# A two-layer encoder trunk on one core: shorter inverse-root chains, and seven-product pairs placed anew in the feed-forward products

## The chip, the cores and the metric

The kernel runs on one core of a Trainium2 chip. The metric is device time in microseconds (us) of one execution; lower is better. A core has five engines with queues of their own: TensorE (PE, with its weight loads PEld), VectorE (DVE), ScalarE (ACT), GpSimd (POOL) and SyncE (SP), which here issues most of the transfers from memory.

## The reference, cut to what matters

256 tokens of width 2048 go through two layers. All is float32. Each layer has an input projection, two kinds of attention, an output projection, and a gated feed-forward part with inner width 5632. Norms stand before and after each part.

```python
def rms_norm(x, g):
    y = xf * lax.rsqrt(jnp.mean(xf * xf, axis=-1, keepdims=True) + EPS)
    return y * g

def swiglu(h, w_gate, w_up, w_down):
    return (jax.nn.silu(h @ w_gate) * (h @ w_up)) @ w_down

for l in range(DEPTH):                      # DEPTH = 2
    h = rms_norm(x, pre_mix_norm[l])
    m = hybrid_mixer(h, l, ...)             # h @ w_in, attention, @ w_o
    x = x + rms_norm(m, post_mix_norm[l])
    h = rms_norm(x, pre_ffn_norm[l])
    f = swiglu(h, w_gate[l], w_up[l], w_down[l])
    x = x + rms_norm(f, post_ffn_norm[l])
return x
```

## The kernel before, in words

**Splitting.** Every float32 factor is written as the sum of two rounded parts, hi and lo. ACT makes hi by a copy (L250), DVE makes lo as the rest (L252). One product of a 128x128 block with a 128x512 block is then three matmuls: hi by hi, hi by lo, lo by hi (function product, L925 to L927; in down also L1135 to L1138, and L1187 to L1189 in its tail).

**Pairs.** Weights arrive in units of 256 rows by 512 columns, one 512 KB load each. A K pair (kp) is 256 rows; there are 8 of them in the input, gate and up products (2048 rows) and 22 in down (5632 rows). The 256 tokens are two tiles of 128 (t = 0, 1). A pair of two weight units (gate and up of one column block, or two column blocks of down) and two token tiles is a 2x2 by 2x2 block product. Done plainly it takes eight products, 24 matmuls. Some pairs are done with seven products, 21 matmuls (seven_products, L942). Such a pair needs sums of weight blocks and of token blocks:

- The weight sums come from mixed_weights (L216). The second unit, T, is loaded by SP and then half of the first unit is added onto it by an accumulating load that POOL issues (L210, L211). DVE then forms a difference in T (L232) and two sums in G (L233), and ACT and DVE split all of it (L225, L226).
- The token sums come from token_sums (L929): four 128x128 operations on DVE and a split (sh on L937, sl on L939). In gate and up, pair_sums (L1028) adds hi and lo first (L1032); the result is kept for all column blocks of the layer.
- Some partial products are shared by several outputs. They go into four banks of their own (p1, p6, p7, q5); after the last seven-product pair of a block, shared_part (L959) moves them to SBUF in one ACT copy and four DVE steps (L963 to L966), which frees the banks.

**Loops.** In the feed-forward part, 11 column blocks c of gate and up run one after the other, each over 8 K pairs. The pairs done with seven products are 2, 4, 5, 6 (SEVEN), in block 0 only 4 and 6 (FIRST_SEVEN, with another order of pairs, FIRST_ORDER). FORM_AT says behind which pair of block 0 the token sums of which pair are built. Then down runs in two halves (two column blocks of 512 each) over 22 pairs; DOWN_SEVEN lists the pairs with seven products, the same in both halves. The last three pairs of half 1 are done by token tile and column block (TAIL), so that tile 0 can be finished while tile 1 is still multiplied.

**Banks.** PSUM has eight banks: four (acc) and four (b and o). Blocks alternate: one set holds a block's sums, the other its shared partial products, and the next block's sums take over the set of the shared products.

**After the products.** evac_chunk (mixer) and evac_sum (down) take a bank's sum, square it with an accumulated total on ACT, and multiply it by the norm's gain on DVE. rescale (L484) adds the four totals, takes the inverse root (rsqrt, L362: logarithm and exponential on ACT, then one Newton step of five DVE operations) and updates x in four blocks of 512 columns (L490). The result is stored (L498) at the end, or transposed for the next part.

**Order.** Loads of weights go in a fixed order through SP's queue, each as soon as its buffer is free: four buffers for ordinary units (raw), three for G, four for T in gate and three in down; six of each split part (hi, lo). A planner orders each engine's queue by priorities; every engine then runs its queue strictly in order.

Of the kernel before, what the change touches and what calls it, by code (L numbers as in the profile page):

```python
# [9 lines left out]
F32 = mybir.dt.float32  # L10
F32R = mybir.dt.float32r
BF16 = mybir.dt.bfloat16
AF = mybir.ActivationFunctionType
# [4 lines left out]
P = 128  # L18
# [32 lines left out]

def lambda_init(layer):
    return 0.8 - 0.6 * math.exp(-0.3 * layer)


def weight_order():

    order = []

    def queue_pair(name, l, kp, c):  # L60
        order.append((name, l, kp, c))
        return len(order) - 1

    plan = []
    sevens, plain = set(), set()
    for l in range(L):
        lay = {"in": {}, "o": {}, "gate": {}, "up": {}, "down": {}}
        for n, (ca, cb) in enumerate(PAIRS):
            for kp in IN_ORDER if n else range(KT // 2):
                lay["in"][ca, kp] = queue_pair("w_in", l, kp, ca)  # L70
                lay["in"][cb, kp] = queue_pair("w_in", l, kp, cb)
                if kp in IN_NOW[n]:
                    plain.add(lay["in"][cb, kp])
        order_o = [(c, kp) for kp in KP_O for c in (0, 1)]
        order_o += [(c, kp) for c in (2, 3) for kp in range(KT // 2)]
        lay["order_o"] = order_o
        for c, kp in order_o:
            lay["o"][c, kp] = queue_pair("w_o", l, kp, c)
        for c in range(FF // CW):
            for kp in FIRST_ORDER if c == 0 else range(KT // 2):  # L80
                lay["gate"][c, kp] = queue_pair("w_gate", l, kp, c)
                lay["up"][c, kp] = queue_pair("w_up", l, kp, c)
                if kp in (FIRST_SEVEN if c == 0 else SEVEN):
                    sevens.add(lay["up"][c, kp])
        for half in range(2):
            for kp in range(FF // P // 2):
                for c in (2 * half, 2 * half + 1):
                    lay["down"][c, kp] = queue_pair("w_down", l, kp, c)
                if kp in DOWN_SEVEN:
# [51 lines left out]
def kernel(  # L141
# [220 lines left out]
    def rsqrt(dst, src, inv, nm):  # L362
        n = dst.shape[-1]
        m = small.tile([P, 2, 4], F32, tag="rsq", bufs=4, name=f"rsq_{nm}")
        u, ms = m[:, 0, 0:n], m[:, 1, 0:n]
        nc.scalar.activation(u, src, AF.Ln, scale=inv, bias=eps)
        nc.scalar.activation(dst, u, AF.Exp, scale=-0.5)
        nc.vector.tensor_scalar(out=ms, in0=src, scalar1=inv, scalar2=EPS, op0=ALU.mult, op1=ALU.add)
        nc.vector.tensor_tensor(out=u, in0=dst, in1=dst, op=ALU.mult)
        nc.vector.tensor_tensor(out=u, in0=u, in1=ms, op=ALU.mult)  # L370
        nc.vector.tensor_scalar(out=u, in0=u, scalar1=-0.5, scalar2=1.5, op0=ALU.mult, op1=ALU.add)
        nc.vector.tensor_tensor(out=dst, in0=dst, in1=u, op=ALU.mult)


    def transposed(t, g0, tiles, cols=range(4)):
# [101 lines left out]
    def evac_sum(pool, acc, mg, ssm, gpost, c, t, nm):  # L477
        m = mg[t, c // 2][:, c % 2, :]
        nc.vector.tensor_tensor(out=m, in0=acc, in1=m, op=shared_sign(t, c % 2))
        junk = pool.tile([P, CW], F32, tag="t2", name=f"jm_{nm}_{t}_{c}")  # L480
        nc.scalar.activation(junk, m, AF.Square, accum_out=ssm[t][:, c : c + 1])
        nc.vector.tensor_tensor(out=m, in0=m, in1=gpost[:, c * CW : (c + 1) * CW], op=ALU.mult)

    def rescale(mg, ssm, t, nm, then=None):  # L484
        tot = small.tile([P, 2], F32, tag="tot", name=f"tot_{nm}_{t}")
        nc.vector.tensor_reduce(out=tot[:, 0:1], in_=ssm[t], axis=AX.X, op=ALU.add)
        rsqrt(tot[:, 1:2], tot[:, 0:1], 1.0 / D, f"{nm}_{t}_p")
        for c in range(4):
            sl = x_part(t, c * CW, CW)
            nc.vector.scalar_tensor_tensor(  # L490
                out=sl, in0=mg[t, c // 2][:, c % 2, :], scalar=tot[:, 1:2], in1=sl, op0=ALU.mult, op1=ALU.add
            )
            if then is not None:
                then(t, c)
# [420 lines left out]
    def load_gain(pool, v, nm, gp=None):  # L915
# [3 lines left out]
            nc.sync.dma_start(gp, v.partition_broadcast(P))  # L919
        return gp  # L920

    def product(a, stat, moving, first, last):
        sh, sl = stat
        hi, lo = moving
        nc.tensor.matmul(a, sh, hi, start=first, stop=False)  # L925
        nc.tensor.matmul(a, sh, lo, start=False, stop=False)  # L926
        nc.tensor.matmul(a, sl, hi, start=False, stop=last)  # L927

    def token_sums(pool, spool, bufs, a11, a12, a21, a22, nm):  # L929

# [41 lines left out]
    for l in range(L):  # L972
# [78 lines left out]

        for c in range(FF // CW):
            banks = four_banks(c % 2, [f"c{q}_{l}_{c}" for q in ("11", "12", "21", "22")])
            mine = FIRST_SEVEN if c == 0 else SEVEN
# [47 lines left out]
        nkp = FF // P // 2  # L1102
        for half in range(2):
            split, forms = {}, {}

            def prep(kp):
                if kp in split or kp >= nkp:
# [7 lines left out]
                if kp in DOWN_SEVEN:  # L1115
# [7 lines left out]
            def down(kp, toks):  # L1123
# [4 lines left out]
                for kk in range(2):  # L1128
                    tick()
                    tick()  # L1130
                    first, last = kp == 0 and kk == 0, kp == nkp - 1 and kk == 1
                    for t in toks:
                        sh, sl = jh[:, kk, t * P : (t + 1) * P], jl[:, kk, t * P : (t + 1) * P]
                        for c, (hi, lo) in zip(cc, ws):
                            nc.tensor.matmul(accs[c, t], sh, hi[:, kk, :], start=first, stop=False)  # L1135
                            nc.tensor.matmul(accs[c, t], sh, lo[:, kk, :], start=False, stop=False)  # L1136
                        for c, (hi, lo) in zip(cc, ws):
                            nc.tensor.matmul(accs[c, t], sl, hi[:, kk, :], start=False, stop=last)  # L1138

            def down_seven(kp):  # L1140
                for n in range(3):
# [5 lines left out]
                seven_products(got, extra, forms[kp], a11, a12, a22, hi, lo, m, kp == DOWN_SEVEN[0], kp == DOWN_SEVEN[-1])  # L1147

            tail = TAIL if half == 1 else 0
            for kp in range(nkp - tail):  # L1150
                if half == 1 and kp == X_BACK:
                    back = [pool.tile([P, 4, S], F32, tag="act", bufs=FF // CW, name=f"xd{l}_{n}") for n in range(4)]
# [5 lines left out]
                if kp not in DOWN_SEVEN:  # L1158
                    down(kp, range(NT))
                    continue  # L1160
                if kp == DOWN_SEVEN[0]:
# [11 lines left out]
            for t in range(NT):  # L1173
# [4 lines left out]
                for c in cc:  # L1178
                    for kp in range(nkp - tail, nkp):
# [4 lines left out]
                        for kk in range(2):  # L1184
                            sh, sl = jh[:, kk, t * P : (t + 1) * P], jl[:, kk, t * P : (t + 1) * P]
                            last = kp == nkp - 1 and kk == 1
                            nc.tensor.matmul(accs[c, t], sh, hi[:, kk, :], start=False, stop=False)  # L1187
                            nc.tensor.matmul(accs[c, t], sh, lo[:, kk, :], start=False, stop=False)
                            nc.tensor.matmul(accs[c, t], sl, hi[:, kk, :], start=False, stop=last)  # L1189
                    with tc.high_priority(offset=URGENT):  # L1190
                        evac_sum(pool, accs[c, t], mg, ssm, gpost, c, t, f"d{l}")
                with tc.high_priority(offset=URGENT):
                    rescale(mg, ssm, t, f"d{l}", store if xT is None else lambda t, c: transposed(t, (l + 1) * KT, xT, cols=(c,)))
# [57 lines left out]
```

## Time and profile before

| | before |
|---|---|
| median of 3 runs | 2213.91 us (2213.34 to 2215.04) |
| the profiled execution | 2215.14 us, of which the span from first to last instruction is 2213.4 us |
| mean granted clock of TensorE | 0.998 |
| DVE, lo of an ordinary unit (L252), x534 | 643.3 us, 1223 ns each |
| DVE, sums in G (L233), x108 | 132.0 us, 1222 ns each |
| matmuls 128x512 in gate and up (L925), x820 | 321.8 us, 395 ns each as drawn |
| loads of ordinary units, x534 | 512 KB each, 4.7 us from issue to landing (median) |
| accumulating loads by POOL, x108 | 256 KB each, 6.7 us (median) |

How to read a page: times are in us from the start of the span unless marked ns. A group's line has the code line, engine and operation, then output<-inputs by the program's names. A bracket at the end of a timeline line has the idle time of the engine just before and what ended it. Matmuls are pipelined and their ends are modelled: one starts before the one before it is drawn as ended.

### The profile page before, as it was taken

Reading aid. Unit: us, or ns where it says so; the run is one execution under the profiler, and the core shown is the slowest. Engines: PE = TensorE matmul, PEld = TensorE weight load, DVE = VectorE, ACT = ScalarE, POOL = GpSimd, SP = SyncE. Lnnn points to the kernel's source line nnn. Section 1 sums busy time; section 2 is a strip of 40 time slices with the busy share of each in tenths; the row PEclk is TensorE's granted clock in tenths of the full one; section 3 lists DMA queues with packets and bytes.
Section 4 is the critical chain, followed back from the end, with each engine's and each line's share of the span. In section 5 each row is a group of like instructions: output and inputs, shape, how many; then the busy total and the mean of one; then the engine's idle time right before and its main releaser. Section 6 shows DMA issues by size and latency. Waiting matters only on the chain.

```text
span 2213.4 us, 28454 instructions
## 1 busy us (share of the span) xinstructions
PE 2185.5 (99%) x10009; PEld 1790.9 (81%) x10009; DVE 1864.0 (84%) x2548; ACT 1354.6 (61%) x2030; POOL 142.2 (6%) x184
## 2 busy tenths in 40 slices
PE   9999999999999999999999999999999999999998
PEld 7788888778888888888888888887788888888886
DVE  7888655899999998989788886559999999999897
ACT  7566664656656656656565656646666556566564
POOL 1200000000000000000011000000000000000000
PEclk9999999999999999999999999999999999999999
DMA  8654555776776775767465545558677677667672
GB/s 304 208 180 153 190 176 186 250 237 215 218 256 211 211 258 180 241 215 240 157 239 190 177 160 177 174 187 268 208 225 235 224 221 238 226 204 243 200 254 98
DMA packets 138079, 466.73 MB, mean 211 GB/s; under 512 B 15824, under 2 KB 16336, under 8 KB 137424
## 3 DMA queue, kind: packets, MB, share of 16 engines
q1 hardware_dynamic: 120512, 430.30, 56.3%
q0 software_dynamic: 15552, 28.32, 7.5%
q10 hardware_dynamic: 1872, 6.31, 0.7%
q8 instruction: 78, 1.28, 0.2%
q14 instruction: 65, 0.53, 0.1%
HBM read 456.47 MB, written 8.39 MB: 210 GB/s over the span
## 4 chain that ended last, share of the span: by engine, by line
PE 78%; DVE 11%; DMA 4%; issue 3%; ACT 3%; SPq 0%; DVEq 0%; ACTq 0%
PE c L925 7%; PE c L926 7%; PE c L927 7%; PE in L925 5%; PE in L927 5%; PE in L926 5%; PE dn L1136 5%; PE dn L1135 5%; PE dn L1138 5%; DVE lo L252 3%; DMA raw<-in_weights_in_turn_dram 3%; PE o L464 3%; PE o L466 3%; PE o L465 3%; DVE Tl L226 2%
## 5 line engine op out<-in xcount | busy, mean ns | idle before, releaser
L252 DVE TENSOR_TENSOR lo<-raw,hi 128x1024 fp32r<-128x1024 f32 x534 | 643.3, 1223 | 161.4 <-ACT hi L250 161.2
L250 ACT ACTIVATE hi<-raw 128x1024 fp32r<-128x1024 f32 x534 | 552.4, 1053 | 235.1 <-DMA raw<-in_weights_in_turn_dram 63.5
L925 PE MATMUL c<-hi,xF 128*128 128x512 f32 x820 | 321.8, 395 | 6.2 <-DVE w L966 4.0
L926 PE MATMUL c<-lo,xF 128*128 128x512 f32 x820 | 320.0, 391 | 0.0
L927 PE MATMUL c<-hi,xF 128*128 128x512 f32 x820 | 318.3, 390 | 0.0
L211 POOL DMA_DIRECT2D T<-in_weights_in_turn_dram x108 | 94.3, 873 | 1669.3 <-PE c L926 520.9
L925 PEld LDWEIGHTS c<-hi,xF 128*128 128x128 f32 x820 | 153.7, 188 | 40.8 <-DVE w L966 6.3
L1135 PE MATMUL dn<-hi,jh 128*128 128x512 f32 x464 | 180.7, 389 | 0.0
L1136 PE MATMUL dn<-lo,jh 128*128 128x512 f32 x464 | 180.5, 389 | 0.0
L926 PEld LDWEIGHTS c<-lo,xF 128*128 128x128 f32 x820 | 154.1, 188 | 32.0 <-DVE lo L252 1.6
L927 PEld LDWEIGHTS c<-hi,xF 128*128 128x128 f32 x820 | 153.9, 188 | 32.1
L252 DVE TENSOR_TENSOR lo<-G,hi 128x1024 fp32r<-128x1024 f32 x108 | 131.7, 1220 | 26.7 <-ACT hi L250 26.6
L225 ACT ACTIVATE Th<-T 128x512 fp32r<-128x512 f32 x108 | 67.8, 627 | 138.6 <-DVE T L232 126.7
L1138 PE MATMUL dn<-hi,jl 128*128 128x512 f32 x464 | 142.9, 389 | 0.0
L226 DVE TENSOR_TENSOR lo<-T,hi 128x1024 fp32r<-128x1024 f32 x108 | 131.7, 1220 | 10.9 <-ACT hi L225 10.3
L226 DVE TENSOR_TENSOR Tl<-G,Th 128x1024 fp32r<-128x1024 f32 x108 | 131.8, 1220 | 9.6 <-ACT Th L225 9.6
L225 ACT ACTIVATE hi<-T 128x1024 fp32r<-128x1024 f32 x108 | 113.4, 1050 | 40.4 <-PE c L927 19.9
L225 ACT ACTIVATE Th<-G 128x1024 fp32r<-128x1024 f32 x108 | 113.9, 1054 | 36.6 <-DVE G L233 35.2
L233 DVE TENSOR_TENSOR G<-G,T 128x1024 f32<-128x1024 f32 x108 | 132.0, 1222 | 2.1
L925 PE MATMUL in<-hi,xT 128*128 128x512 f32 x328 | 131.5, 402 | 0.5 <-ACT hi L738 0.5
L925 PE MATMUL in<-hi,xI 128*128 128x512 f32 x328 | 131.3, 402 | 0.2 <-ACT xI L383 0.2
L926 PE MATMUL in<-lo,xT 128*128 128x512 f32 x328 | 128.2, 391 | 1.0 <-DVE lo L252 0.8
(376 smaller groups left out, 4660.2 us busy)
## 6 DMA issues: line engine op xcount, KB each, us to landing
raw<-in_weights_in_turn_dram SPq DMA_DIRECT2D x534, 512.0 KB, 4.7
T<-in_weights_in_turn_dram SPq DMA_DIRECT2D x108, 512.0 KB, 4.7
G<-in_weights_in_turn_dram SPq DMA_DIRECT2D x108, 512.0 KB, 4.8
T<-in_weights_in_turn_dram POOLq DMA_DIRECT2D x108, 256.0 KB, 6.7
GU<-in_weights_in_turn_dram SPq DMA_DIRECT2D x32, 512.0 KB, 4.6
away_ffn<-x ACTq DMA_DIRECT2D x8, 512.0 KB, 6.1
xd<-away_ffn SPq DMA_DIRECT2D x8, 512.0 KB, 9.2
xr<-in_x_columns_dram SPq DMA_DIRECT2D x8, 256.0 KB, 6.7
```

The lines of the kernel that those rows point to most:

```text
L211: nc.gpsimd.dma_start(sums[i][:, 0, :], stream[i - 1][:, 0, :], accum_op=ALU.add)
L225: nc.scalar.activation(h, w, AF.Copy)
L226: nc.vector.tensor_tensor(out=l, in0=w, in1=h.bitcast(F32), op=ALU.subtract)
L233: nc.vector.tensor_tensor(out=g, in0=g, in1=t2.unsqueeze(1).to_broadcast([P, 2, CW]), op=ALU.add)
L250: nc.scalar.activation(hi, raw, AF.Copy)
L252: rest = nc.vector.tensor_tensor(out=lo, in0=raw, in1=hi.bitcast(F32), op=ALU.subtract)
L925: nc.tensor.matmul(a, sh, hi, start=first, stop=False)
L926: nc.tensor.matmul(a, sh, lo, start=False, stop=False)
L927: nc.tensor.matmul(a, sl, hi, start=False, stop=last)
L1135: nc.tensor.matmul(accs[c, t], sh, hi[:, kk, :], start=first, stop=False)
L1136: nc.tensor.matmul(accs[c, t], sh, lo[:, kk, :], start=False, stop=False)
L1138: nc.tensor.matmul(accs[c, t], sl, hi[:, kk, :], start=False, stop=last)
```

## The change

It has five parts.

1. DOWN_SEVEN becomes two lists, one for each half, of seven pairs each instead of six: 4, 7, 10, 12, 15, 17, 20 in half 0 and 3, 5, 8, 10, 13, 15, 18 in half 1. Before it was 3, 6, 9, 12, 15, 18 in both.
2. Column block 1 of gate and up does pairs 4, 5, 6 with seven products (NEXT_SEVEN) and pair 2 with eight. The token sums of pair 2 are built in block 1 behind its pair 3, not in block 0.
3. rsqrt scales the mean by -0.5 at once and joins operations, so its Newton step takes two DVE operations after the mean for a single column and three for four columns, where it took four.
4. rescale no longer calls rsqrt. It adds the first three totals early, gives them to the logarithm as its bias and the fourth total as its input, and ends with the two Newton operations.
5. In half 1 of down in the last layer, token tile 1's shared partial products are added into the PSUM banks as soon as they are known, while matmuls are still to come there. Its evacuation then squares the bank itself, and multiplies the bank by the gain. The last block of 512 columns is scaled and stored in two parts of 256.

```diff
-FORM_AT = {1: 4, 2: 6, 4: 5, 5: 2}
-DOWN_SEVEN = (3, 6, 9, 12, 15, 18)
+NEXT_SEVEN = (4, 5, 6)
+FORM_AT = {(0, 1): 4, (0, 2): 6, (0, 5): 5, (1, 3): 2}
+DOWN_SEVEN = ((4, 7, 10, 12, 15, 17, 20), (3, 5, 8, 10, 13, 15, 18))
...
+def gate_sevens(c):
+
+    return (FIRST_SEVEN, NEXT_SEVEN)[c] if c < 2 else SEVEN
...
-        nc.vector.tensor_scalar(out=ms, in0=src, scalar1=inv, scalar2=EPS, op0=ALU.mult, op1=ALU.add)
+        nc.vector.tensor_scalar(out=ms, in0=src, scalar1=-0.5 * inv, scalar2=-0.5 * EPS, op0=ALU.mult, op1=ALU.add)
+        if n == 1:
+            newton(dst, u, ms)
+            return
         nc.vector.tensor_tensor(out=u, in0=dst, in1=dst, op=ALU.mult)
         nc.vector.tensor_tensor(out=u, in0=u, in1=ms, op=ALU.mult)
-        nc.vector.tensor_scalar(out=u, in0=u, scalar1=-0.5, scalar2=1.5, op0=ALU.mult, op1=ALU.add)
-        nc.vector.tensor_tensor(out=dst, in0=dst, in1=u, op=ALU.mult)
+        nc.vector.scalar_tensor_tensor(out=dst, in0=u, scalar=1.5, in1=dst, op0=ALU.add, op1=ALU.mult)
+
+    def newton(y, u, ms):
+
+        nc.vector.scalar_tensor_tensor(out=u, in0=y, scalar=ms, in1=y, op0=ALU.mult, op1=ALU.mult)
+        nc.vector.scalar_tensor_tensor(out=y, in0=u, scalar=1.5, in1=y, op0=ALU.add, op1=ALU.mult)
...
+        if summed:
+            junk = pool.tile([P, CW], F32, tag="t2", name=f"jm_{nm}_{t}_{c}")
+            nc.scalar.activation(junk, acc, AF.Square, accum_out=ssm[t][:, c : c + 1])
+            nc.vector.tensor_tensor(out=m, in0=acc, in1=gpost[:, c * CW : (c + 1) * CW], op=ALU.mult)
+            return
...
-        nc.vector.tensor_reduce(out=tot[:, 0:1], in_=ssm[t], axis=AX.X, op=ALU.add)
-        rsqrt(tot[:, 1:2], tot[:, 0:1], 1.0 / D, f"{nm}_{t}_p")
+        nc.vector.tensor_reduce(out=three, in_=ssm[t][:, 0:3], axis=AX.X, op=ALU.add)
+        nc.vector.tensor_scalar(out=most, in0=three, scalar1=1.0 / D, scalar2=EPS, op0=ALU.mult, op1=ALU.add)
+        nc.vector.tensor_scalar(out=half, in0=three, scalar1=-0.5 / D, scalar2=-0.5 * EPS, op0=ALU.mult, op1=ALU.add)
+        nc.scalar.activation(u, fourth, AF.Ln, scale=1.0 / D, bias=most)
+        nc.scalar.activation(r, u, AF.Exp, scale=-0.5)
+        nc.vector.tensor_scalar(out=ms, in0=fourth, scalar1=-0.5 / D, scalar2=half, op0=ALU.mult, op1=ALU.add)
+        newton(r, u, ms)
         for c in range(4):
+            if halves and c == 3:
+                for a in (0, CW // 2):
+                    sl = x_part(t, c * CW + a, CW // 2)
+                    nc.vector.scalar_tensor_tensor(
+                        out=sl, in0=mg[t, 1][:, 1, a : a + CW // 2], scalar=r, in1=sl, op0=ALU.mult, op1=ALU.add
+                    )
+                    nc.sync.dma_start(ov[t][:, c * CW + a : c * CW + a + CW // 2], sl)
+                continue
...
             for n, kp in enumerate(order):
-                if c == 0 and n in FORM_AT:
+                if (c, n) in FORM_AT:
                     with after_rests():
-                        pair_sums(FORM_AT[n])
+                        pair_sums(FORM_AT[c, n])
...
         for half in range(2):
+            mine = DOWN_SEVEN[half]
...
             tail = TAIL if half == 1 else 0
+            open_sums[0] = half == 1 and l + 1 == L
...
-                if kp == DOWN_SEVEN[-1]:
+                if kp == mine[-1]:
                     for t in range(NT):
                         mg[t, half] = dn.tile([P, 2, CW], F32, tag="qk", bufs=4, name=f"mg_d{l}_{t}_{half}")
                     shared_part(extra, [mg[t, half][:, j, :] for t in range(NT) for j in range(2)])
+                    if open_sums[0]:
+                        for c in cc:
+                            nc.vector.tensor_tensor(out=accs[c, 1], in0=accs[c, 1], in1=mg[1, half][:, c % 2, :], op=shared_sign(1, c % 2))
```

The lines left out replace SEVEN, FIRST_SEVEN and DOWN_SEVEN by the new lists where they were used, and give the matmuls into those banks a flag that lets them go on after the addition.

More of the change, by code (lines that the diff above doesn't have):

```diff
@@ L482, in evac_sum, with rescale @@
         nc.vector.tensor_tensor(out=m, in0=m, in1=gpost[:, c * CW : (c + 1) * CW], op=ALU.mult)
-    def rescale(mg, ssm, t, nm, then=None):
-        tot = small.tile([P, 2], F32, tag="tot", name=f"tot_{nm}_{t}")
-        nc.vector.tensor_reduce(out=tot[:, 0:1], in_=ssm[t], axis=AX.X, op=ALU.add)
-        rsqrt(tot[:, 1:2], tot[:, 0:1], 1.0 / D, f"{nm}_{t}_p")
-        for c in range(4):
+    def rescale(mg, ssm, t, nm, then=None, halves=False):
+        tot = small.tile([P, 6], F32, tag="tot", name=f"tot_{nm}_{t}")
+        three, most, half, ms, u, r = (tot[:, j : j + 1] for j in range(6))
+        fourth = ssm[t][:, 3:4]
+        nc.vector.tensor_reduce(out=three, in_=ssm[t][:, 0:3], axis=AX.X, op=ALU.add)
[5 more added lines that the diff above has]
+        newton(r, u, ms)
+        for c in range(4):
+            if halves and c == 3:
[6 more added lines that the diff above has]
+                continue
             sl = x_part(t, c * CW, CW)
             nc.vector.scalar_tensor_tensor(
-                out=sl, in0=mg[t, c // 2][:, c % 2, :], scalar=tot[:, 1:2], in1=sl, op0=ALU.mult, op1=ALU.add
+                out=sl, in0=mg[t, c // 2][:, c % 2, :], scalar=r, in1=sl, op0=ALU.mult, op1=ALU.add
             )
@@ L924, in product @@
         hi, lo = moving
-        nc.tensor.matmul(a, sh, hi, start=first, stop=False)
-        nc.tensor.matmul(a, sh, lo, start=False, stop=False)
-        nc.tensor.matmul(a, sl, hi, start=False, stop=last)
+        nc.tensor.matmul(a, sh, hi, start=first, stop=False, skip_group_check=open_sums[0])
+        nc.tensor.matmul(a, sh, lo, start=False, stop=False, skip_group_check=open_sums[0])
+        nc.tensor.matmul(a, sl, hi, start=False, stop=last, skip_group_check=open_sums[0])
     def token_sums(pool, spool, bufs, a11, a12, a21, a22, nm):
@@ L1134, in down @@
                         for c, (hi, lo) in zip(cc, ws):
[L1135 to L1136 removed]
+                            nc.tensor.matmul(accs[c, t], sh, hi[:, kk, :], start=first, stop=False, skip_group_check=open_sums[0])
+                            nc.tensor.matmul(accs[c, t], sh, lo[:, kk, :], start=False, stop=False, skip_group_check=open_sums[0])
                         for c, (hi, lo) in zip(cc, ws):
[L1138 removed]
+                            nc.tensor.matmul(accs[c, t], sl, hi[:, kk, :], start=False, stop=last, skip_group_check=open_sums[0])
             def down_seven(kp):
```

27 lines of the change are left out of this document (14 added, 13 removed).

## The prediction

> **What bounds the kernel now.** I read the page's busy times, then TensorE's waits, then the timeline and chain around the longest wait, then the busy time by stage, then the tail.
>
> ```profile
> PE 2185.5 (99%) x10009; PEld 1790.9 (81%) x10009; DVE 1864.0 (84%) x2548; ACT 1354.6 (61%) x2030; POOL 142.2 (6%) x184
> ```
>
> PE is busy nearly everywhere. In the timeline full matmuls start 0.227 us apart though each is drawn 0.39 us long, so one matmul more or less is 0.227 us where nothing else is late. What PE waited for:
>
> ```profile
> PE c L925 <- DVE w L966: 4.0, 2, 2.1
> PE p L925 <- ACT Th L225: 2.0, 2, 1.0
> PE p L926 <- DVE Tl L226: 1.6, 4, 0.6
> ...
> PE p_d L926 <- DVE Tl L226: 1.0, 1, 1.0
> ...
> PE q L925 <- ACT sh L937: 0.7, 2, 0.4
> ```
>
> Columns: total us, times, longest. Idle is counted from the drawn end of a matmul, so each stall costs 0.16 us (0.39 - 0.227) more than shown. The timeline puts them once in each layer: w at 494 and 1594 us, Th and sh at 460 to 465 and 1561 to 1565 us, Tl at 440, 611, 1540 and 1712 us. All lie in the first gate/up column blocks. The longest, on VectorE:
>
> ```profile
> 488.67 0.68 DVE L963 TENSOR_TENSOR w<-p,w 128x512 f32<-128x512 f32 x1
> 489.30 1.23 DVE L252 TENSOR_TENSOR lo<-raw,hi 128x1024 fp32r<-128x1024 f32 x1
> 490.44 0.68 DVE L964 TENSOR_TENSOR w<-p,w 128x512 f32<-128x512 f32 x1
> 493.87 1.23 DVE L252 TENSOR_TENSOR lo<-raw,hi 128x1024 fp32r<-128x1024 f32 x1 [2.74 <-ACT hi L250]
> 495.01 0.68 DVE L965 TENSOR_TENSOR w<-q,w 128x512 f32<-128x512 f32 x1
> 495.61 0.68 DVE L966 TENSOR_TENSOR w<-q,w 128x512 f32<-128x512 f32 x1
> ```
>
> The reader is to see a queue in order: the last two steps that free block 1's shared banks stand behind a weight split whose load is late, and block 2 needs those banks. The chain of waits says why it is late:
>
> ```profile
> 485.37 7.33 DMA raw<-in_weights_in_turn_dram
> 492.78 1.07 ACT hi L250
> ```
>
> The load was issued only when an earlier split (a late VectorE) gave back its buffer, and took 7.33 us. So VectorE is the bound from about 419 to 496 us and PE later. By stage (steady gate/up, then down):
>
> ```profile
> 620.00:880.00 260.00, 260.00 (x1175) 215.39 (x1174) 243.30 (x268) 160.01 (x185) 19.22 (x22) 1.00 0.68 216
> 880.00:1100.00 220.00, 218.95 (x968) 181.01 (x967) 191.07 (x248) 134.17 (x176) 8.72 (x10) 1.00 0.67 215
> ```
>
> Third field PE, fifth DVE. Gate/up at 94% DVE keeps PE full; down has DVE at 87%. The tail:
>
> ```profile
> 2203.54 0.69 DVE L479 TENSOR_TENSOR mg_d<-dn,mg_d 128x512 f32<-128x512 f32 x1 [0.32 <-PE dn L1189]
> 2205.02 0.16 DVE L486 TENSOR_REDUCE tot_d<-ssm_d 128x1 f32<-128x4 f32 x1 [0.79 <-ACT jm_d L481]
> 2206.35 0.16 DVE L372 TENSOR_TENSOR tot_d<-tot_d,rsq_d_p 128x1 f32<-128x1 f32 x1
> 2206.54 2.74 DVE L490 SCALAR_TENSOR_TENSOR xd<-mg_d,tot_d,xd 128x512 f32<-128x512 f32 x4
> ```
>
> 3.04 us pass from the last matmul's end (2203.50) to the first scaled block, 2.74 for four blocks, about 4.1 for the last store and the end.
>
> **The change, part by part.**
>
> *Products.* Down gets one more pair of seven products in each of 4 halves: 4 x 3 = 12 matmuls fewer. Gate block 1 loses one in each layer: 6 more. Net -6 x 0.227 = **-1.4 us**.
>
> *Gate blocks 0 and 1.* A seven-product pair costs VectorE, beyond the two splits of an ordinary pair, T (0.69), G (1.22) and two Tl (0.69, 1.22): 3.8 us by durations, 3.5 by distance of starts (1.135 and 0.60). That leaves block 1, and the forms of pair 2 (about 2.1 us) move from block 0 into block 1, where pairs 2 and 3 are now ordinary. VectorE's work between 419 and the end of L966 shrinks from 496.2 to about 492.7 us even if the 2.74 wait stays, and to 490 without it; the instruction order of the new kernel has only one late-loaded split ahead of the third bank step, not two. PE, without the stalls at 460 to 465 (0.51 + 1.17) and with three more matmuls (0.68), reaches the bank at about 494.1 - 1.0 = 493. So w, Th and sh should go: 6.7 + 6 x 0.16 = 7.7 us. I take **-7.0**; the bounds are 0 and -7.7. Late next is Tl of block 0 (440 and 1540 us), whose cover hardly changes: it stays. The two Tl stalls near 611 and 1712 (about 1.3 with the 0.16) come from the same lag: **-0.5**, bounds 0 and -1.3.
>
> *Down.* The p_d wait is half 0's first seven pair in layer 0, waiting for a late T (its split waited 4.74 us on VectorE at 884). It moves from pair 3 to pair 4, 24 x 0.227 = 5.4 us later: **-1.2**, bounds 0 and -1.2. A pair more costs VectorE 3.5 + 1.4 (four 128x128 sums 0.20 apart, one sl 0.60) = 4.9 us; over five pairs with two of seven, VectorE needs 2 x 7.7 + 3 x 2.87 = 24.1 us against PE's (2 x 21 + 3 x 24) x 0.227 = 25.9: 93%, the gate's level, so hidden. POOL issues four more accumulating loads here, two fewer in gate; SP's loads change in order, not in number (one store more at the very end). The cover is thin where half 0 ends: its last seven pair moves from 18 to 20, so one pair (5.4 us) instead of three lies between it and half 1, which writes first into the banks that the shared part frees. From pair 17 to pair 5 of half 1 VectorE needs 4 x 7.7 + 7 x 2.87 + 5.0 (the half's evacuation, 987.64 to 992.61) + 2.4 (shared part) = 58.3 us against PE's 4 x 4.76 + 7 x 5.44 = 57.1, and in the new order two splits stand between the bank steps, as at 490 us. Bounds: 0, and 2.26 (the stall at 494) in each layer, 4.5; nearer 0, since VectorE had been waiting for PE there (0.33 us): **+1.0**.
>
> *Tail.* Token tile 1's shared part is added into the PSUM banks early: two 128x512 operations that the trace lacks (0.69 as L479 to 1.22 as the dearest split), done after 2190.7 and needed by PE at 2195.3 (36 x 0.227 before 2203.5), so hidden; without cover 1.4 us. After the last matmul: square and accumulator read (0.68), bank times gain (0.60), the mean (0.20), two Newton steps (0.19 each) and hand-overs (0.07) are 1.93 us, against 3.04. The steps on 128x1 are of a form not shown; bounds 0.16 (TENSOR_TENSOR 128x1) and 0.34 (the smallest scalar_tensor_tensor, 128x128), nearest 0.16. The gain product waits for the square as in the mixer's evacuation, which does the same two reads of a bank:
>
> ```profile
>   ACT jm_o L471: 9.4, 6
> ```
>
> (what L475 waited for: us, times). The Trainium skill, "PSUM — Partial Sum Buffer", section "PSUM bank collisions raise a hardware error", says that no two engines may touch one bank at once, reads included; the trace agrees by that wait. Were it not so the two reads would overlap and 0.15 us more be gained.
>
> The halved last block costs what it saves (0.36 + 0.42 against 0.74); its store has half the bytes: 0 to 0.3, I take 0.2. Tail **-1.3**, bounds -0.8 and -1.6.
>
> *Other roots.* Two or one fewer 128x1 operations each, hidden beside other work inside the layers. At the three layer seams the chain is about 0.4 to 0.6 shorter, but PE's transposes also stand up to 7 matmuls earlier in its queue at 1104 us, so a late block stops PE longer: **-0.4**, bounds -1.5 and +1.5.
>
> **Sum**: -1.4 - 7.0 - 0.5 - 1.2 + 1.0 - 1.3 - 0.4 = -10.8. Against the profiled span 2213.4: 2202.6. That execution took 2215.14 (1.7 around the span), 1.2 above the median 2213.91 of the runs; against the median, **2203.1**. With all bounds at their best (-14.7) 2199.2; at their worst (+3.8) 2217.7.
>
> **Rivals.**
>
> *Down turns late.* The half's seam pays the whole 4.5 us, and the closest pairs, three short gaps in each half 1, a stall of Tl's size (0.6 + 0.16) once in each of the two: 1.5. For: the sums of 93% and 102% above. Against: gate keeps PE full at 94%. 2203.1 + 3.5 + 1.5 = 2208.1, still faster.
>
> *The gate stalls stay.* They follow from the load's 7.33 us and not from VectorE's lag: one late split is still ahead of the second bank step. Then 7.0 + 0.5 are not gained: 2210.6, within 0.2%. Against: the load waits for a buffer that VectorE frees.
>
> *Slower.* SP issues in order, and T and G have three buffers each in down (four T in gate). Where sevens stand two pairs apart, a T or G whose buffer is not free holds the ordinary loads queued behind it, and each such place pays the 2.26 us of the stall at 494. There are 5 such places in a layer (10-12, 15-17, 3-5, 8-10, 13-15), 10 in all: +22.6, 2225.7. It decides from 1.08 us a place (10.8 / 10). For: SP's waits in down are already on VectorE. Against: three sevens in a row in gate run without such stalls, and buffer three is five pairs old.
>
> That the change does nothing of this kind is out: the built order shows 110 instead of 108 T and G sums and 12 down matmuls fewer.
>
> **How the numbers follow.** Forecast 0.64 (own range 2199 to 2207), down late 0.17, gate stalls stay 0.13, slower 0.06. 0.2% (4.4 us) is about what a measurement of this kernel can tell from no change. Faster 0.64 + 0.17 = 0.81, same 0.13, slower 0.06. The range reaches from a little under the best sum, 2198.5, to the stalls that stay, 2210.6; the slower case and a part of the third are left out.
>
> **What would show it.** PE's wait list without w L966, Th and sh of block 1 and without p_d; Tl of block 0 still there; PE free of waits at the end of half 0 or under 1 us each; first scaled block 1.9 us after the last matmul; VectorE about 92% in down. A p_d or dn wait on L1001's line, or raw loads late behind T in down, would prove me wrong, as would a w wait that stays.

## The result and the profile after

The changed kernel takes **2208.56 us** (median of 10 runs, 2207.69 to 2211.12) against 2213.35 for the kernel before (10 runs on the same chip, 2210.72 to 2215.04). The ratio is 0.9978, 95% interval 0.9970 to 0.9986: 4.8 us faster, where 10.8 were forecast. The profiled execution took 2208.14 us, 1.7 of it around its span of 2206.4.

The busy times of the changed kernel, and the first rows of what TensorE waited for (total us, times, longest):

```profile
PE 2182.1 (99%) x10003; PEld 1791.1 (81%) x10003; DVE 1871.3 (85%) x2545; ACT 1362.6 (62%) x2038; POOL 140.2 (6%) x186
```

```profile
PE p L961 <- DVE Tl L232: 2.4, 6, 0.6
PE c L961 <- DVE lo L258: 2.2, 2, 1.7
PE c L960 <- DVE w L1001: 1.7, 2, 0.8
PE xT_ps L393 <- DVE xd L523: 1.4, 1, 1.4
...
PE c L960 <- DVE w L999: 1.0, 3, 0.4
```

Six matmuls fewer, as announced (10003 for 10009). Gone are sh of block 1 and the p_d wait, and Th of block 1 is down from 1.0 to 0.2 in each layer. The wait for the last bank step, 4.0 in two before, is 1.7 in two, and its longest fell from 2.1 to 0.8. But Tl grew from four to six, and two are new: a matmul of gate that waits for an ordinary weight split (L258), and one wait of the transposes between the layers.

To see where the time went, the span is cut at the first matmul of each stage, from the timelines. "opening" is all that stands ahead of the first layer's output product. "layer 1" is the stage from the first matmul of the second layer's input product to that of its output product, and contains the seam between the layers. "tail" begins with the start of the last matmul. The rows below the second are the kernels of the experiments. Times in us, one profile each; worked out, not a view of the profile:

```
                 opening gate/up 0 down 0 layer 1 gate/up 1 down 1  tail   span
before            302.09   471.71  234.34  296.36   471.98  231.90 10.32 2213.4
changed           300.29   471.30  231.81  297.65   470.06  230.52  9.77 2206.4
old gate          301.62   471.33  231.83  299.39   473.81  230.52  9.76 2213.3
old down          302.50   471.25  234.50  297.81   469.43  233.17  9.69 2213.4
only gate         301.34   471.08  234.06  296.39   470.09  231.87 10.34 2209.9
only down         301.49   470.91  231.64  296.56   472.85  230.54 10.35 2209.1
only roots, tail  300.65   472.50  234.49  297.85   473.37  232.75  9.72 2216.4
old roots, tail   300.70   472.69  231.64  295.69   469.81  230.54 10.29 2206.1
rsqrt only        301.06   471.47  234.49  298.07   470.09  232.72 10.17 2212.6
loads' room       300.45   469.25  231.83  298.58   468.27  230.57  9.67 2203.7
old seam          300.62   470.66  231.62  296.25   468.92  230.54  9.69 2203.3
spread            300.77   467.56  231.81  297.42   467.35  230.52  9.69 2200.2
better, first     300.92   468.66  231.62  295.98   468.14  230.51  9.36 2199.9
better, second    300.54   469.63  231.64  295.94   467.30  230.52  9.39 2200.0
```

(The two output stages, 97.4 each, are left out.) In the opening the change touches only small roots. It varies by 2.2 us from profile to profile, and not by the roots (300.7 to 302.1 with the old ones, 300.3 to 302.5 with the new); that is most of why the spans differ by 7.0 and the medians by 4.8. Without the opening the changed kernel gains 5.2: gate/up 0.4 + 1.9, down 2.5 + 1.4, tail 0.55, less 1.3 in layer 1 and 0.3 in the output stages. Gate/up has noise of its own: only down leaves it as it was, and there the two stages came out 0.8 shorter and 0.9 longer than before.

**Why gate/up gained so little.** TensorE's stalls moved more than they went. Summed over the waits of more than 0.1 us, each as the distance of the two starts less 0.227, they came to 6.8 and 6.4 us in the two gate/up stages before and to 6.5 and 5.5 in the changed kernel: 1.3 us less, where 7.5 were forecast.

The busy time of each engine in the stretch up to the last bank step of block 1, first before, then changed (fields: stretch, length, PE, PE's weight loads, DVE, ACT, POOL, granted clock, share of the DMA engines, GB/s):

```profile
419.00:496.30 77.30, 72.97 (x317) 58.00 (x317) 72.61 (x98) 47.20 (x55) 6.94 (x8) 1.00 0.82 258
```

```profile
417.40:493.70 76.30, 72.69 (x315) 57.33 (x315) 68.77 (x93) 43.97 (x52) 6.07 (x7) 1.00 0.82 265
```

VectorE did lose 3.8 us of work here (the forecast was 3.5 and more), but its idle time rose from 4.7 to 7.5 us, and the stretch is only 1.0 shorter. What it idled for, in the timeline of VectorE and of ScalarE in the changed kernel:

```profile
457.72 0.69 DVE L974 TENSOR_TENSOR sl<-s,sh 128x512 fp32r<-128x512 f32 x1 [1.84 <-ACT sh L972]
458.33 3.49 DVE L258 TENSOR_TENSOR lo<-raw,hi 128x1024 fp32r<-128x1024 f32 x3
...
485.62 0.69 DVE L998 TENSOR_TENSOR w<-p,w 128x512 f32<-128x512 f32 x1
489.99 1.23 DVE L258 TENSOR_TENSOR lo<-raw,hi 128x1024 fp32r<-128x1024 f32 x1 [3.68 <-ACT hi L256]
491.13 0.68 DVE L999 TENSOR_TENSOR w<-p,w 128x512 f32<-128x512 f32 x1
491.74 0.68 DVE L1114 TENSOR_TENSOR w<-c,w 128x512 f32<-128x512 f32 x1
492.33 0.68 DVE L1000 TENSOR_TENSOR w<-q,w 128x512 f32<-128x512 f32 x1
492.93 0.68 DVE L1001 TENSOR_TENSOR w<-q,w 128x512 f32<-128x512 f32 x1
```

```profile
456.11 1.06 ACT L256 ACTIVATE hi<-raw 128x1024 fp32r<-128x1024 f32 x1 [2.35 <-DMA raw<-in_weights_in_turn_dram]
457.07 0.61 ACT L972 ACTIVATE sh<-s 128x512 fp32r<-128x512 f32 x1
...
488.90 1.06 ACT L256 ACTIVATE hi<-raw 128x1024 fp32r<-128x1024 f32 x1 [7.64 <-DMA raw<-in_weights_in_turn_dram]
```

Both are queues in order behind a late load. At 457 ScalarE stands at a split whose load is late; the token sums' sh is queued behind it, VectorE stands at their sl, and behind sl stand three weight splits, one of which TensorE waits for (1.88 us lost). At 489 it is the load that the prediction saw. The chain of waits shows it again, issued when a split gave its buffer back at 481:

```profile
481.19 7.60 DMA raw<-in_weights_in_turn_dram
488.90 1.07 ACT hi L256
```

7.60 us, where 7.33 stood before, though VectorE had less to do. Counted from the first gate matmul (399.45 us before, 397.81 now), the load was issued 2.5 us sooner (83.4 for 85.9) and landed 2.3 us sooner (91.0 for 93.2): the lag did give way. The last bank step (L1001) still ended only 1.0 us sooner (95.8 for 96.8), because of the new order of VectorE's queue. Three bank steps and one other operation (L1114) now stand behind the late split, where before two bank steps stood behind it.

### The profile page after: what moved, and what is told of

The parts are those of the page before. It is cut to its first block, busy times and chain, and to the rows that moved or that the text cites. A ratio compares the mean times of both kernels' runs of the same rounds, so it can differ in the third digit from the quotient of the medians.

```text
span 2206.4 us, 28457 instructions
## 1 busy us (share of the span) xinstructions
PE 2182.1 (99%) x10003; PEld 1791.1 (81%) x10003; DVE 1871.3 (85%) x2545; ACT 1362.6 (62%) x2038; POOL 140.2 (6%) x186
## 4 chain that ended last, share of the span: by engine, by line
PE 86%; DVE 7%; issue 2%; ACT 2%; DMA 2%; SPq 0%; DVEq 0%; ACTq 0%
PE c L960 9%; PE c L961 9%; PE c L962 9%; PE in L960 6%; PE in L962 6%; PE in L961 6%; PE dn L1172 4%; PE dn L1174 4%; PE dn L1171 4%; PE o L479 3%; PE o L477 3%; PE o L478 3%; PE p L961 2%; PE p L962 2%; PE p L960 2%
## 5 line engine op out<-in xcount | busy, mean ns | idle before, releaser
L258 DVE TENSOR_TENSOR lo<-raw,hi 128x1024 fp32r<-128x1024 f32 x530 | 638.9, 1223 | 157.3 <-ACT hi L256 156.4
L960 PE MATMUL c<-hi,xF 128*128 128x512 f32 x834 | 328.3, 396 | 3.9 <-DVE w L1001 1.7
L961 PE MATMUL c<-lo,xF 128*128 128x512 f32 x834 | 325.6, 390 | 2.2 <-DVE lo L258 2.2
L962 PE MATMUL c<-hi,xF 128*128 128x512 f32 x834 | 325.0, 391 | 0.0
L217 POOL DMA_DIRECT2D T<-in_weights_in_turn_dram x110 | 95.8, 871 | 1688.9 <-DMA T<-in_weights_in_turn_dram 547.2
L960 PEld LDWEIGHTS c<-hi,xF 128*128 128x128 f32 x834 | 156.3, 188 | 38.9 <-ACT hi L256 3.0
L962 PEld LDWEIGHTS c<-hi,xF 128*128 128x128 f32 x834 | 156.5, 188 | 32.6
L1171 PE MATMUL dn<-hi,jh 128*128 128x512 f32 x432 | 168.4, 390 | 0.0
L1172 PE MATMUL dn<-lo,jh 128*128 128x512 f32 x432 | 168.3, 390 | 0.0
L258 DVE TENSOR_TENSOR lo<-G,hi 128x1024 fp32r<-128x1024 f32 x110 | 134.3, 1221 | 34.4 <-ACT hi L256 34.3
L1174 PE MATMUL dn<-hi,jl 128*128 128x512 f32 x432 | 133.0, 390 | 0.0
L961 PE MATMUL in<-lo,xI 128*128 128x512 f32 x328 | 128.1, 391 | 0.5 <-DVE lo L258 0.5
```

Of the source, the lines that this page charges most:

```text
L217: nc.gpsimd.dma_start(sums[i][:, 0, :], stream[i - 1][:, 0, :], accum_op=ALU.add)
L258: rest = nc.vector.tensor_tensor(out=lo, in0=raw, in1=hi.bitcast(F32), op=ALU.subtract)
L960: nc.tensor.matmul(a, sh, hi, start=first, stop=False, skip_group_check=open_sums[0])
L961: nc.tensor.matmul(a, sh, lo, start=False, stop=False, skip_group_check=open_sums[0])
L962: nc.tensor.matmul(a, sl, hi, start=False, stop=last, skip_group_check=open_sums[0])
```

## The experiments

Times are medians; ratios are to the kernel before, run on the same chip. The changed kernel was not run again beside them, and on the three chips used here the kernel before took 2212.35 to 2214.04 us, so a difference of medians to the changed kernel is sure to within 1 to 2 us only. The ratio of the changed kernel, 0.9978, can be compared without that.

**One part undone or alone.** "old gate" and "old down" put back these lists in the changed kernel, "only roots" has both put back:

```diff
-NEXT_SEVEN = (4, 5, 6)
-FORM_AT = {(0, 1): 4, (0, 2): 6, (0, 5): 5, (1, 3): 2}
+NEXT_SEVEN = (2, 4, 5, 6)
+FORM_AT = {(0, 1): 4, (0, 2): 6, (0, 4): 5, (0, 5): 2}
...
-DOWN_SEVEN = ((4, 7, 10, 12, 15, 17, 20), (3, 5, 8, 10, 13, 15, 18))
+DOWN_SEVEN = ((3, 6, 9, 12, 15, 18), (3, 6, 9, 12, 15, 18))
```

> The changed kernel with gate/up as before (block 1 with pairs 2, 4, 5, 6 by seven products, all forms in block 0). By the prediction's theory (VectorE's lag was all that stood behind the stalls) the gate edit is worth 6.5 us, so this run is 6.5 us above the changed kernel, 2215. By the rival (block 1's eight ordinary units in a row are limited by four ordinary load buffers and a load time of 5 to 7.6 us, so that the edit only trades one stall for another) it is 0 to 2.3 us above it, 2208.5 to 2211, the gate/up stages take 471.5 and 471.8 us as in the kernel before (471.1 and 469.8 in the changed one), and TensorE's waits on w (2.1 us) and Th come back while the 1.7 us wait on lo goes.

2213.68, ratio 0.9997 (0.9988 to 1.0006). With the other parts in place the gate edit is worth 5.1 us by the medians, which is nearer to the prediction's 6.5 than to the rival's 0 to 2.3. The waits are those that the rival named: w and Th come back, the one on lo goes. By the stages gate/up of the first layer does not change; 3.8 lie in gate/up of the second layer, and 1.7 in layer 1, where the input product, which the edit leaves alone, stops 2.1 us for an ordinary split. So this run does not decide between the two; room for two loads, below, does.

> The changed kernel with down as before (six pairs in each half at 3, 6, 9, 12, 15, 18). If down gave what its matmuls say, the two down stages are 2.1 and 1.4 us longer than in the changed kernel (231.6 and 230.5) and the run is 3.5 us above it, 2212. If the denser pairs had cost time that hides in other stages, it is less than 2 us above.

2213.11, ratio 0.9996 (0.9988 to 1.0005). Down is worth 4.6 us in these surroundings by the medians, 5.3 by its two stages, more than forecast.

> Only the shorter inverse roots and the new tail; gate/up and down as in the kernel before. By the prediction 1.7 us under the kernel before (tail -1.3, seams -0.4). By the rival (transposes stand earlier in TensorE's queue at the seam between the layers, and the halved last store costs more than it saves) tail -0.6, seam between the layers +0.8, together 0 within 1 us, with a TensorE wait on xd of over 1 us at the seam.

2217.22, ratio 1.0013 (1.0004 to 1.0022): **3.4 us slower than before**, where the prediction had 1.7 faster and the rival no change within 1 us. The table says where: 1.5 in layer 1, 0.9 in down 1, 0.8 and 1.4 in gate/up, for 0.6 from the tail. Its waits:

```profile
PE c L960 <- ACT w L997: 1.9, 2, 1.0
PE p_d L961 <- DVE Tl L232: 1.5, 2, 1.0
...
PE xT_ps L393 <- DVE xd L523: 1.3, 1, 1.3
```

The first is new, at the start of gate block 1 in each layer; p_d comes twice instead of once; the third is the seam.

**The gate's sevens spread out.** Block 1 does pairs 2, 4, 6 with seven products instead of 4, 5, 6: the same count, but no run of four ordinary pairs, each with two loads through the four ordinary buffers.

```diff
-NEXT_SEVEN = (4, 5, 6)
-FORM_AT = {(0, 1): 4, (0, 2): 6, (0, 5): 5, (1, 3): 2}
+NEXT_SEVEN = (2, 4, 6)
+FORM_AT = {(0, 1): 4, (0, 2): 6, (0, 5): 2, (1, 3): 5}
```

> The changed kernel with block 1's three seven-product pairs at 2, 4, 6 instead of 4, 5, 6 (token sums of pair 2 in block 0, of pair 5 in block 1 behind its pair 3). TensorE and VectorE do as much as in the changed kernel. By the theory of VectorE's lag it takes the same time, 2208.5 within 1 us. By the rival (loads through four ordinary buffers) T and G units stand between the ordinary ones, the 1.9 us stall on lo at 457 us and part of the one on w at 491 us go, in both layers: 3 to 6 us less, 2202.5 to 2205.5.

2204.91, ratio 0.9955 (0.9942 to 0.9967): 3.7 us under the changed kernel by the medians, and the intervals of the two ratios lie apart. Gate/up falls to 467.6 and 467.4, TensorE's stalls in it to 2.6 and 2.7. The edit moves more than loads (T and G units and token sums change places too); the next run moves loads alone. ScalarE's wait for ordinary loads between 430 and 500 us, changed kernel, then this one:

```profile
ACT hi L256 <- DMA raw<-in_weights_in_turn_dram: 18.3, 6, 7.6
```

```profile
ACT hi L256 <- DMA raw<-in_weights_in_turn_dram: 7.7, 4, 4.2
```

**Room for two loads.** Nothing is computed otherwise; pair 2 of block 1 is loaded into two buffers that seven-product pairs use.

```diff
+    roomy = {}
+    for lay in plan:
+        roomy[lay["gate"][1, 2]], roomy[lay["up"][1, 2]] = "G", "T"
...
+            if i in roomy:
+                tag, bufs = roomy[i], mix_raw[1] if roomy[i] == "G" else mix_raw[2]
+                raw = mix_raw[0].tile([P, 2, CW], F32, tag=tag, bufs=bufs, name=f"{tag}{i}")
```

> The changed kernel, but the two raw weight units of pair 2 in block 1 of gate and up go into two of the G and T buffers that seven-product pairs use, and not into the four ordinary buffers; same products, same VectorE work, same order. If the stalls at 457 us (1.9 and 0.4) and their like come from loads held by the four buffers: 1 to 2 us less in each layer, about 2206. If they come from VectorE's lag (the prediction's cause): no change, 2208.5.

2206.47, ratio 0.9956 (0.9944 to 0.9968), an interval apart from the changed kernel's. By the stages gate/up gains 2.05 and 1.8. The first rows of what TensorE waited for between 400 and 620 us, first the changed kernel, then this one:

```profile
PE c L961 <- DVE lo L258: 1.7, 1, 1.7
PE p L961 <- DVE Tl L232: 1.2, 3, 0.5
PE c L960 <- DVE w L1001: 0.8, 1, 0.8
```

```profile
PE p L967 <- DVE Tl L238: 1.2, 3, 0.5
PE c L966 <- DVE w L1007: 0.8, 1, 0.8
```

The wait at 457 is gone with the buffers alone: VectorE's work is the same. The waits for bank steps at 489 to 492 stay (0.7 and 1.0 us lost, 0.6 and 1.0 in the changed kernel), and so does the load behind them (not one of the two that were moved):

```profile
487.20 1.06 ACT L262 ACTIVATE hi<-raw 128x1024 fp32r<-128x1024 f32 x1 [7.78 <-DMA raw<-in_weights_in_turn_dram]
```

**What the roots cost, and where.** "no roots" is the changed kernel with the old root, scaling and tail (parts 3 to 5 of the change undone; in the table "old roots, tail"). "rsqrt only" is the kernel before with the new rsqrt and the old rescale. "old seam" is the changed kernel, in which only the scaling after the first layer's down and the norm behind it keep the old chain:

```diff
     def rescale(mg, ssm, t, nm, then=None, halves=False):
+        if nm == "d0":
+            rescale_old(mg, ssm, t, nm, then)
+            return
...
-        rsqrt(rs[:, 0:1], ss, 1.0 / D, f"{nm}_{t}")
+        (rsqrt_old if nm == "in1" else rsqrt)(rs[:, 0:1], ss, 1.0 / D, f"{nm}_{t}")
```

> The changed kernel with the inverse roots, the scaling of rows and the tail as before; new places of sevens in gate and down stay. The prediction (roots -0.4, tail -1.3) says 1.7 us slower than the changed kernel: 2210.3. The theory that the shorter roots cost (only_roots measured +3.35 over before: transposes of the layer seam issued earlier and held by a late block 1.5 us, first gate blocks 0.8 and 1.4 later, down 0.85) says about 3.3 us faster: 2205.2, with the seam stage back near 296.4 and the tail back to 10.3. A third, that the +3.35 came only with the old places of sevens: 2208.5, no change.

2208.18, ratio 0.9965 (0.9953 to 0.9977). By the medians that is the third of the expectations, no change. By the ratios (0.9978 for the changed kernel) it is 2.9 us faster, near the second, but the intervals overlap. So in these surroundings the roots and the tail cost between nothing and 3 us. By the stages they cost 2.0 in layer 1 and 0.3 in the output stages, for 0.5 in the tail and 1.1 in gate/up, which is near that stage's noise. The p_d waits and those at the start of block 1, which they cost in the old places of sevens, don't arise.

> The kernel before with the shorter inverse root alone (the general one and that of one column), scaling of rows and tail as before. It tells the two parts of only_roots (+3.35) apart. If the general root (queries and keys in the mixer, and the two of the norms) brings the cost: 2215 to 2217. If the new scaling of rows brings it: 2213.9, as before. By the prediction: 2213.5 to 2213.9.

2214.99, ratio 0.9999 (0.9990 to 1.0008): no change. Layer 1 is 1.7 longer and down 1 0.8. The second p_d wait (0.7 us) comes with the root alone. Layer 1 is longer by other waits than in the changed kernel: 0.7 at the seam, for the transposed block and not for the scaled one, and 1.9 at 1137 us for ordinary splits of the input product. Of the waits at the start of block 1 (L997; L982 here) one of 0.4 us is left, so they belong for the most part to the new scaling with the old gate.

> The changed kernel with the old chain of inverse roots at the seam between the layers alone (scaling of rows after the first layer's down, and the norm of the second layer's input); all else as changed. In the built order TensorE's transposes then stand as in the kernel before: among the last blocks one by one, not four in a row. If the 1.5 us stall at the seam comes from that early place: the stage that holds the seam falls from 297.7 to about 296, and the time by 1.5 to 2 us from 2208.6 to about 206.8 over 2000, that is 2206.8. If it comes from the load-bound opening of the second layer or is a matter of the run: no change, 2208.5.

2206.78, ratio 0.9974 (0.9963 to 0.9984). Layer 1 falls from 297.65 to 296.25. TensorE at the seam, first the changed kernel, then this one:

```profile
1108.81 1.53 PE L393 MATMUL xT_ps<-ident,xd 128*128 128x128 f32 x12 [1.35 <-DVE xd L523]
```

```profile
1107.57 0.66 PE L405 MATMUL xT_ps<-ident,xd 128*128 128x128 f32 x4 [0.30 <-DVE rsq_d_p L377]
```

Twelve transposes in a row, at which TensorE loses 1.5 us, become blocks of four with matmuls between them, and 0.5 is lost. The shorter chain does what it should (the root of token tile 1 is ready 6.2 us after the tile's last matmul starts, 9.1 before), but the new order has TensorE there after 6.6 us, and VectorE has the block ready after 8.1. The time is 1.8 under the changed kernel by the medians and 0.9 by the ratios; the intervals overlap, so the stage carries the verdict. It agrees over all profiles: layer 1 takes 295.7 to 296.6 us in the seven kernels with the old chain at this seam and 297.4 to 299.4 in the seven with the new root there. A wait on xd of 1.3 to 1.4 us stands in all six with the new root and the new scaling there, and in no other.

**Gate and down alone.** The kernel before with the changed gate lists, and with the changed down list: of the first diff above, the lines marked with a minus go into the kernel before, one list at a time.

> The kernel before with the new sevens of gate and up alone (blocks 0 and 1, places of the forms). By the prediction's sum: +1.4 for six matmuls more, -7.5 for the stalls: 6.1 under before. If the stalls only move, since the loads wait for four buffers: the two gate stages gain 2 to 2.5 together and the time 2 to 3.

2211.58, ratio 0.9993 (0.9983 to 1.0002). The gate stages gain 0.6 and 1.9: 2.5, not 6.1. The time alone can't be told from no change. Four pairs of kernels in the table differ in these lists alone (before and only gate, only roots and old down, only down and old roots, old gate and changed). In gate/up of the first layer the new lists gain 0.6, 1.2, -1.8 and 0.0 us, in the second 1.9, 3.9, 3.0 and 3.8: together 3.2 in the mean, from 1.3 to 5.2.

> The kernel before with the seven pairs of seven products in each half of down alone. By the prediction's sum: -2.7 for twelve matmuls, -1.2 for the wait of the first pair, +1.0 for the seam of the halves: 2.9 under before. If the seam of the halves costs nothing, as the changed kernel's stages show: 3.9 under before. If down turned late here: no gain.

2210.57, ratio 0.9992 (0.9983 to 1.0001), 1.8 by the medians and not to be told from no change by the interval; the two down stages gain 2.7 and 1.4, 4.1 together, and gate/up in the second layer came out 0.9 longer with nothing changed there.

**Towards a better kernel.** Both have the spread sevens of gate, the new down, and the last block in one piece. The first has the old roots and scaling except in half 1 of the last layer's down, the second the new ones except at the seam.

```diff
+        if not open_sums[0]:
+            rescale_old(mg, ssm, t, nm, then)
+            return
...
-            if halves and c == 3:
+            if False:
```

> Sevens of block 1 at pairs 2, 4, 6; down as in the changed kernel; inverse roots and scaling as before everywhere but in the last token tile, which keeps the shorter chain and the early addition into the banks, without the halved last block. If the roots cost inside the layers and gain at the tail, 2204.9 (spread sevens) less 3 to 4: about 2201. If the roots cost nothing in this surrounding, the time of the spread kernel, 2205, or up to 1.2 more by the prediction's sum.

2202.05, ratio 0.9938 (0.9926 to 0.9950).

> Sevens of block 1 at pairs 2, 4, 6, the old chain at the seam between the layers alone, the shorter chain elsewhere, the last block in one piece; down as changed. By the stages of the runs so far: gate 467.5 in each layer, the seam's stage 296, the tail 9.4, so 1.5 to 2 for the seam and 0.4 for the tail under the 2204.9 of the spread kernel: about 2202.5, or 2200.2 by the sum of the best stages. If the seam's stall is not the early place: 2204.5.

2202.06, ratio 0.9955 (0.9943 to 0.9968). Their tails are 9.36 and 9.39, where 9.67 to 9.77 stand with the halved block. Neither can be told from the other, nor by span from spread (2199.9, 2200.0, 2200.2); all three beat both kernels by their ratios. A stall of 1.25 and 1.77 us at 483 us (a wait for Th) takes back in gate/up of the first layer part of what the seam gives (first and second kernel).

## Why the prediction was wrong

In the order of its sum, with what the stages of the changed kernel show:

- *Products.* Six matmuls fewer at 0.227: right. In down 1, where nothing waited before, the stage is shorter by 1.38, which is 6 x 0.227.
- *Gate blocks 0 and 1* (-7.0, near Tl -0.5, and +1.4 for its six matmuls: -6.1; measured -2.3). **This step failed and is 3.8 of the 5.5 us that are missing** by these two profiles; by the mean of the four pairs it would be 2.9. It said that the stalls follow from VectorE's lag, so that less work there lets w, Th and sh go. VectorE's work did shrink by 3.8 us and the late load was issued 2.5 us sooner, but the last bank step ended only 1.0 us sooner after the first gate matmul (95.8 for 96.8; forecast 93.3 at the latest). The load's 7.33 us stayed, at 7.60. The prediction counted one late split instead of two ahead of the third bank step, which is so, and overlooked that this one stands ahead of the second step, with three steps behind it. And turning pair 2 ordinary put a run of four ordinary pairs, eight loads, through four buffers: the stall at 457 is of the edit's own making, as room for two loads and spread show. Sh did go, Th shrank to 0.35 and w to 0.60 + 1.00; Tl, forecast to fade at 611 us, is there earlier, at 506 and 528 (0.71 and 0.58).
- *Down* (-2.7, p_d -1.2, seam of the halves +1.0: -2.9; measured -3.9). Right but for the seam of the halves, which cost nothing: no p_d and no dn wait is left, with VectorE 92% busy, as forecast:

```profile
869.00:1100.00 231.00, 231.00 (x1029) 191.33 (x1028) 213.27 (x289) 148.89 (x196) 12.19 (x14) 1.00 0.69 224
```

  Old down showed more (4.6) because the new roots bring a second p_d wait with the old places.
- *Tail* (-1.3; measured -0.55). The first scaled block comes 2.11 us after the last matmul, forecast 1.93, before 3.04: the chain was sized about right. Mis-sized was the halved last block, taken as 0.2 of gain: it costs 0.3 to 0.4, as the tails of the last two runs show. Its second part is issued 5.15 us after the last matmul's end, where the whole block is issued after 4.89 (better, second), and takes 0.2 us more to land. These rows of the changed kernel give operation, KB each, and the median from issue to landing:

```profile
out_dram<-xd SPq DMA_DIRECT2D x7, 256.0 KB, 2.8
...
out_dram<-xd SPq DMA_DIRECT2D x2, 128.0 KB, 3.1
```

  Half the bytes land no sooner. The Trainium skill, "DMA: Bandwidth & Descriptors", section "Anatomy of one DMA — SWDGE (gpsimd) path", puts most of a small transfer's time into a fixed part of about 2.0 us, for another issuing path than this one. By its fit, with bytes / 436e3 on top, half of 256 KB would save 0.3 us (an estimate from that page); the rows here show no saving. The gain product did wait for ScalarE's square of the same bank, as the prediction drew from the mixer and from the Trainium skill, "PSUM — Partial Sum Buffer", section "PSUM bank collisions raise a hardware error":

```profile
2197.81 0.69 DVE L495 TENSOR_TENSOR mg_d<-dn,gpost_ffn 128x512 f32<-128x512 f32 x1 [2.37 <-ACT jm_d L494]
```

- *Other roots* (-0.4, bounds ±1.5; measured +1.6 in layer 1 and the output stages). **The second step that failed.** The prediction saw the transposes move up and gave a longer stop of TensorE as the upper bound, but it counted on a small gain. What decides is that they come twelve in a row, 6.6 us after the last matmul of token tile 1 starts, while the block is scaled only after 8.1. Of the pairs of kernels that differ in the roots and the tail alone, all four show it: layer 1 is longer by 1.4 to 2.8 us.

Of the rivals, "the gate stalls stay" (2210.6) names the mechanism (one late split still ahead of the second bank step), though it is half of it: sh and most of Th went, and new stalls came. "Down turns late" (2208.1) comes near the time by the wrong way: no wait is left in down, not even where sevens stand two pairs apart, which refutes "slower" too.

What stays open: why the load at 481 to 488 us takes 7.3 to 7.8 us where it is late. The trace of the changed kernel points to the loads in flight beside it. Three were in flight when it was issued, and five more were issued before it landed, SP's 1.14 us apart, while it and SP's next four landed 1.3 to 2.0 us apart. Over gate/up and down of that kernel, a weight load from SP took 3.2 us (median) when no other weight load was in flight at its issue, 5.0 with two, 6.7 with four and 7.9 with six (worked out from issues and landings). No run changed this alone. How much of the differences of 0.9 us and less in gate/up is the loads' chance is open as well.

## What to carry to other kernels

When an engine that works in order is both late and fed by loads, taking work from it gives back only what the loads allow. Count the loads that the edit puts one after another through the same buffers, read what stands behind the late item in each queue, and treat the time of a late load as a given until a run shows otherwise. Where some items load through other buffers than the rest, spread them among the rest; a run of items that all share one small set of buffers makes its own stall. A shorter dependency chain can cost time where a scheduler reorders another engine's queue by it, so read the new order at each seam as closely as the durations.

## What was unexpected on the chip

- A store of 128 KB lands after 3.1 us, one of 256 KB after 2.8; halving the last one lengthened the tail by 0.3 to 0.4.
- The ordinary weight load has a median of 4.6 us to landing, but the one issued at 481 us in the changed kernel needed 7.6 with less work on VectorE, and with room for two other loads its like still took 7.7.
- The opening, the same in all kernels but for small roots, took 300.3 to 302.5 us in the profiles, and a gate/up stage left as it was differed by 0.9: differences under about 1 us in one stage of one profile say little here.
